# Compressed blocks laid side by side in SBUF, written by ScalarE and VectorE instead of by DMA, in a hybrid attention decoder block

## The chip, the core and the metric

The kernel runs on one NeuronCore of a Trainium2 chip. The metric is the device time of one execution in microseconds (us), from start to end of the program. Of the engines, TensorE (PE) multiplies matrices, and its weight loads are listed apart as PEld; VectorE (DVE), ScalarE (ACT) and GpSimd (POOL) do elementwise work; SyncE (SP) issues most DMAs. A few runs of the same kernel are taken and their median is given; one further execution is profiled.

## The reference

One decoder layer for 512 tokens of width 1024: an RMS norm, one input projection, an attention group and a gated short convolution group side by side, an output projection, and then a gated MLP with a short convolution. The attention group has 8 query heads, 2 key/value groups and three branches. The part that the change touches is the compressed branch: keys and values are cut into 31 overlapping blocks of 32 tokens (a new one every 16 tokens), a position table `pe` is added, and each block goes through a small MLP whose first layer has 32 x 64 inputs.

```python
def compress_kv(kv, pe, w1, w2):
    B, S, G, dh = kv.shape
    n_cmp = (S - L_CMP) // S_CMP + 1                      # 31
    idx = jnp.arange(n_cmp)[:, None] * S_CMP + jnp.arange(L_CMP)[None, :]
    blk = kv[:, idx] + pe[None, None, :, None, :]
    blk = blk.transpose(0, 3, 1, 2, 4).reshape(B, G, n_cmp, L_CMP * dh)
    return jax.nn.gelu(blk @ w1, approximate=True) @ w2

    kc = compress_kv(k_c, pe_k, wk1, wk2)
    vc = compress_kv(v_c, pe_v, wv1, wv2)
    logits_c = jnp.einsum('bgrsd,bgnd->bgrsn', qg, kc) * scale + tab[:, :, t5_bucket(dist_c)]
    p_c = masked_softmax(logits_c, dist_c >= 0)
    o_c = jnp.einsum('bgrsn,bgnd->bgrsd', p_c.astype(vc.dtype), vc)
```

All inputs and outputs are float32.

## The kernel before

Float32 precision is kept with pairs: `split` (L132) writes a tile as `hi`, a copy rounded to float32r by ACT (L134), and `lo`, the rest, by a subtraction on DVE (L135). A product is then the sum of hi times hi, lo times hi and hi times lo. Weights arrive through `Stream` (L55): a load of 512 KB on SP's queue into one of three `raw` tiles (L73), then a split on ACT (L85) and DVE (L88) into one of four `ring` tiles.

The kernel's order is: a start-up that normalizes and projects keys, values and two query groups; then the attention steps with projection steps filled in between (`fill`, L564), in the order written out in `ORDER` (L44); the output projection; the MLP's up-projection (line `pu`) and down-projection (line `z`). In the filled part `c0` and `c1` project the 128 columns (2 groups x 64) of keys and values for compression; `q2` and `q3` are query projections; `h0` to `h7` are the first layer of the compression MLP; `g`, `x` and `b` belong to the short convolution; `s` is the second layer of the compression MLP. The instructions of an engine run in a fixed order, which the framework sets when the program is built.

The code around the change:

- `blocks(kv, p)` (L425) runs after `c0` and after `c1`. `normed` (L370) takes the projection out of PSUM into a tile of tag `t2` (three buffers), on DVE (L372). One `split` of 128x512 makes `hl`, hi and lo, in two more `t2` buffers. Then eight DMAs on SP's queue (L435) copy pieces of `hl` into X, one for each half of a token pair (`lp`), group `g` and `s` (hi or lo). The last 16 tokens of group 0 don't go to X but to `tails`, by two small splits (L431).
- X holds, on partition `lp*64 + d`, value `d` of token `t + lp`, in the order kv, hi/lo, group, token: tokens side by side. Tokens `2*l2` and `2*l2 + 1` of a block lie on the two halves of the partitions, so that 16 steps of `l2` cover a block's 32 tokens.
- `hidden_steps(c)` (L443) does the first layer: for each `l2` and `kv` the stationary operand `xs` (L453) is taken from X: 4 (hi/lo, group) times 32 (block) columns, 16 elements apart. The moving operand is 256 columns of the weights, first hi, then lo. That is 16 x 2 x 2 = 64 matmuls (L457), each with its own weight load, all into the bank `ph`.
- The position table is carried as a 32nd block of group 0, whose result is later added as a bias (`peb`, L477). In the first half of the steps the places of this block hold `pes[:, :, :, :8]`; before `c == 4`, `halves()` (L437) puts the tails back and writes the second half of the table into the beginning of group 1.

Of the kernel before, what the change touches and what calls it, by code (L numbers as in the profile page):

```python
# [22 lines left out]
F32R = mybir.dt.float32r  # L23
# [4 lines left out]
S = 512  # L28
D = 1024
P = 128  # L30
NT = S // P
KT = D // P
HD = 64
NH = 8
NG = 2
NB = 32
NCMP = 31
# [13 lines left out]
def f32(ap):  # L51
    return ap.bitcast(F32)
# [58 lines left out]
def block_kernel(ctx: ExitStack, tc: tile.TileContext, a, out):  # L111
    nc = tc.nc
# [4 lines left out]
    const = ctx.enter_context(tc.tile_pool(name="const", bufs=1))  # L117
# [14 lines left out]
    def split(hi, lo, src):  # L132

        act(hi, src, AF.Copy)  # L134
        nc.vector.tensor_tensor(lo, src, f32(hi), op=ALU.subtract)  # L135
# [13 lines left out]
    for what in ORDER.split():  # L149
        name, _, count = what.partition(":")  # L150
# [24 lines left out]
    opool = opool_cm.__enter__()  # L175
    ph1_cm = tc.tile_pool(name="ph1", bufs=1)
    ph1 = ph1_cm.__enter__()
# [168 lines left out]
    for n in range(2):  # L346
        nc.sync.dma_start(UR[:, 4 * n:4 * n + 4, :], bass.AP(tensor=vd.tensor, offset=vd.offset + n * 4 * 640,
                                                             ap=[[1, P], [640, 4], [1, S]]))
# [21 lines left out]
    def normed(p, name):  # L370
        t = t2(name)[:, :S]
        nc.vector.tensor_tensor(t, p, Rb, op=ALU.mult)  # L372
        return t
# [38 lines left out]

    X = opool.tile([P, 4 * 1024 + 16], F32R, tag="o16", name="X")
    Xv = X[:, :4096].rearrange("p (v s g t) -> p v s g t", v=2, s=2, g=NG)
    nc.gpsimd.memset(f32(X[:, 4096:]), 0.0)
    pes = const.tile([P, 2, 2, 16], F32R, name="pes")  # L420
    split(pes[:, :, 0], pes[:, :, 1], peT)
    tails = const.tile([P, 2, 2, 8], F32R, name="tails")
    nc.vector.tensor_copy(Xv[:, :, :, 0, 496:512:2], f32(pes[:, :, :, :8]))

    def blocks(kv, p):  # L425
        p = normed(p, f"ct{kv}")
        hl = [ph1.tile([P, 520], F32R, tag="t2", bufs=3, name=f"x{s}{kv}")[:, :S] for s in range(2)]
        split(hl[0], hl[1], p)
        for lp in range(2):
            half = slice(lp * HD, (lp + 1) * HD)  # L430
            split(tails[half, kv, 0], tails[half, kv, 1], p[:HD, 496 + lp:512:2])  # L431
            for g in range(NG):
                n = S - lp if g else 496
                for s in range(2):
                    nc.sync.dma_start(f32(Xv[half, kv, s, g, :n]), f32(hl[s][g * HD:(g + 1) * HD, lp:lp + n]))  # L435

    def halves():  # L437
        nc.vector.tensor_copy(Xv[:, :, :, 0, 496:512:2], f32(tails))
        nc.vector.tensor_copy(Xv[:, :, :, 1, 0:16:2], f32(pes[:, :, :, 8:]))

    phs = {}

    def hidden_steps(c):  # L443

        if c == 0:
            phs[0] = mm_bank("ph")
        w = W.next()
        if c == 4:
            halves()
        for l in range(2):  # L450
            l2 = 2 * c + l
            for kv in range(2):
                xs = bass.AP(tensor=X.tensor, offset=X.offset + kv * 2048 + 2 * l2, ap=[X.ap[0], [512, 4], [16, 32]])  # L453
                for s in range(2):
                    cc = slice(l * 512 + kv * 256, l * 512 + kv * 256 + 256)

                    MM(phs[0][:, kv * 256:kv * 256 + 256], xs, w[:, s, cc],  # L457
                       start=l2 == 0 and kv == 0 and s == 0, stop=l2 == 15 and kv == 1 and s == 1)
            yield
# [37 lines left out]
    def c_steps(kv):  # L497
        p = mm_bank(f"pp_c{kv}")
        yield from proj_steps(p, W.next())
        blocks(kv, p)  # L500
# [39 lines left out]
    def b_steps(c):  # L540
# [3 lines left out]
        split(oTc[:, 0, c, :], oTc[:, 1, c, :], ct[c])  # L544

    kinds = {"q": q_steps, "h": hidden_steps, "g": g_steps, "x": x_steps, "b": b_steps}

    def work():
# [28 lines left out]
    def compressed_softmax(i):  # L577
# [10 lines left out]
        m = const.tile([P, NH], F32, tag="cm", bufs=2, name=f"cm{i}")  # L588
        nc.vector.tensor_reduce(m, zv, axis=AX.X, op=ALU.min)
        nc.vector.tensor_tensor(zv, zv, m[:, :, None].to_broadcast([P, NH, nv]), op=ALU.subtract)  # L590
        act(zv, zv, AF.Exp, scale=-1.0)
        sm = const.tile([P, NH], F32, tag="csm", bufs=2, name=f"csm{i}")
        nc.vector.tensor_reduce(sm, zv, axis=AX.X, op=ALU.add)
        nc.vector.reciprocal(sm, sm)
# [263 lines left out]
    for n, m in enumerate(UP):  # L858
# [7 lines left out]
        if m >= NF:  # L866
            f = m - NF
# [97 lines left out]
```

## Time and profile before

| what | us |
|---|---|
| median of 3 runs (632.74 to 636.84) | 634.15 |
| the profiled execution | 633.81 |
| its span, from the first to the last instruction | 632.0 |
| PE busy | 622.0 |
| weight loads busy | 517.8 |
| DVE busy | 372.9 |
| ACT busy | 305.3 |
| POOL busy | 42.8 |

The mean granted TensorE clock is 0.996 of full speed. Busy times of PE and of its weight loads overlap each other. Matmuls are pipelined: one begins before the one ahead of it ends, so that the time that a matmul costs in a row of them is the distance from start to start and not its duration. A window is a stretch of the span, in us from its start. In the chain of waits, work is followed back from the last instruction, at each step to what released it.

### The profile page before, as it was taken

The numbers are of one execution on the slowest core, as the hardware profiler recorded it, in microseconds if no ns is written. First come the engines' busy times: TensorE is split into PE (matmuls) and PEld (weight loads), VectorE is DVE, ScalarE is ACT, GpSimd is POOL, SyncE is SP. The second block draws the span as 40 slices with busy tenths as digits, with TensorE's granted clock in tenths as the row PEclk, the third lists the DMA queues.
The fourth block names the chain that finished last, engine by engine and source line by source line (L and its number), as shares of the span: only waits on it lengthen the run. The fifth ranks groups of instructions, "written<-read, shape, count | busy, mean of one in ns | idle before, by whom it ended". The sixth has DMA issues, their size and how long they took to land.

```text
span 632.0 us, 8054 instructions
## 1 busy us (share of the span) xinstructions
PE 622.0 (98%) x2980; PEld 517.8 (82%) x2980; DVE 372.9 (59%) x665; ACT 305.3 (48%) x562; POOL 42.8 (7%) x90
## 2 busy tenths in 40 slices
PE   8999999999999999999999999999999999999995
PEld 7888898878878788898888888888888888888884
DVE  4677756689988746647656566665656542222224
ACT  5757735589998736346433444343443321222212
POOL 1200002003020203200000000000000000000001
PEclk9999999999999999999999999999999999999998
DMA  8976555201112573014222222332332223222103
GB/s 312 337 207 200 146 186 167 69 18 41 45 42 76 169 263 134 1 34 133 101 100 96 87 91 96 100 101 100 101 100 101 98 102 98 92 87 90 67 10 124
DMA packets 26295, 71.45 MB, mean 113 GB/s; under 512 B 3368, under 2 KB 8040, under 8 KB 26256
## 3 DMA queue, kind: packets, MB, share of 16 engines
q1 hardware_dynamic: 25968, 70.65, 33.9%
q8 instruction: 23, 0.38, 0.2%
q10 hardware_dynamic: 288, 0.29, 0.1%
q14 instruction: 16, 0.13, 0.1%
HBM read 64.88 MB, written 2.12 MB: 106 GB/s over the span
## 4 chain that ended last, share of the span: by engine, by line
PE 94%; DVE 2%; DMA 1%; ACT 1%; POOL 0%; SPq 0%; issue 0%; DVEq 0%; POOLq 0%; ACTq 0%
PE pu L170 13%; PE pu L171 13%; PE pu L169 13%; PE z L770 6%; PE z L769 6%; PE z L771 6%; PE sc L620 3%; PE y L770 2%; PE y L771 2%; PE y L769 2%; PE tr L649 2%; PE ph L457 2%; PE o L657 1%; PE o L658 1%; PE pcg L169 1%; PE pcg L171 1%
## 5 line engine op out<-in xcount | busy, mean ns | idle before, releaser
L169 PE MATMUL pu<-h2T,w_u 128*128 128x512 f32 (+1 forms) x384 | 142.8, 372 | 0.0
L170 PE MATMUL pu<-h2T,w_u 128*128 128x512 f32 (+1 forms) x384 | 142.6, 371 | 0.0
L171 PE MATMUL pu<-h2T,w_u 128*128 128x512 f32 (+1 forms) x384 | 142.6, 371 | 0.0
L169 PEld LDWEIGHTS pu<-h2T,w_u 128*128 128x128 f32 x384 | 72.3, 188 | 12.6
L170 PEld LDWEIGHTS pu<-h2T,w_u 128*128 128x128 f32 x384 | 72.3, 188 | 12.5
L171 PEld LDWEIGHTS pu<-h2T,w_u 128*128 128x128 f32 x384 | 72.3, 188 | 12.4
L853 DVE SCALAR_TENSOR_TENSOR cv<-pu,ffnw,cv 128x511 f32<-128x511 f32 x44 | 32.9, 749 | 70.2 <-ACT cv L852 70.2
L88 DVE TENSOR_TENSOR w_d<-raw_d,w_d 128x1024 fp32r<-128x1024 f32 x22 | 26.9, 1224 | 72.8 <-ACT w_d L85 72.8
L769 PE MATMUL z<-w_d,aT 128*128 128x512 f32 x176 | 68.5, 389 | 0.0
L770 PE MATMUL z<-w_d,aT 128*128 128x512 f32 x176 | 68.5, 389 | 0.0
L771 PE MATMUL z<-w_d,aT 128*128 128x512 f32 x176 | 68.5, 389 | 0.0
L852 ACT ACTIVATE cv<-pu,ffnw 128x512 f32<-128x512 f32 x44 | 30.3, 688 | 64.0 <-PE pu L171 63.9
L85 ACT ACTIVATE w_d<-raw_d 128x1024 fp32r<-128x1024 f32 x22 | 23.3, 1059 | 75.2 <-PE z L771 75.2
L88 DVE TENSOR_TENSOR w_u<-raw_u,w_u 128x1024 fp32r<-128x1024 f32 x44 | 53.4, 1216 | 5.9 <-ACT w_u L85 5.8
L85 ACT ACTIVATE w_u<-raw_u 128x1024 fp32r<-128x1024 f32 x44 | 46.2, 1052 | 6.6 <-PE pu L171 6.3
L626 ACT ACTIVATE P<-P,mins 128x512 f32<-128x512 f32 (+3 forms) x64 | 35.4, 554 | 7.8 <-DVE mins L624 7.4
L769 PEld LDWEIGHTS z<-w_d,aT 128*128 128x128 f32 x176 | 33.0, 188 | 6.9
L771 PEld LDWEIGHTS z<-w_d,aT 128*128 128x128 f32 x176 | 33.0, 188 | 6.9
L770 PEld LDWEIGHTS z<-w_d,aT 128*128 128x128 f32 x176 | 33.0, 188 | 6.7
L134 ACT ACTIVATE aT<-cv 128x512 fp32r<-128x512 f32 x22 | 13.9, 631 | 49.4 <-DVE cv L870 49.4
L854 DVE SCALAR_TENSOR_TENSOR cv<-pu,ffnw,cv 128x510 f32<-128x510 f32 x44 | 32.8, 748 | 1.5
L624 DVE CUSTOM_DVE_ANT_0 P<-sc,UR 128x512 f32<-128x512 f32 (+3 forms) x64 | 30.1, 482 | 2.6 <-PE sc L620 1.7
(221 smaller groups left out, 1111.3 us busy)
## 6 DMA issues: line engine op xcount, KB each, us to landing
raw_u<-in_w_u SPq DMA_DIRECT2D x44, 512.0 KB, 3.2
raw_d<-in_w_d SPq DMA_DIRECT2D x22, 512.0 KB, 3.2
raw_c<-in_w_c SPq DMA_DIRECT2D x8, 512.0 KB, 3.3
raw_o<-in_w_o SPq DMA_DIRECT2D x8, 512.0 KB, 3.4
xT<-in_xT SPq DMA_DIRECT2D x8, 256.0 KB, 5.1
xt<-in_x SPq DMA_DIRECT2D x4, 512.0 KB, 4.8
raw_q<-in_w_t SPq DMA_DIRECT2D x4, 512.0 KB, 6.3
UR<-vd SPq DMA_DIRECT2D x2, 1024.0 KB, 8.3
```

What stands on the lines that cost most here:

```text
L85: self.nc.scalar.activation(t[:, 0, c:c + step], self.raws[n][:, c:c + step], AF.Copy)
L88: eng.tensor_tensor(t[:, 1, cs], self.raws[n][:, cs], f32(t[:, 0, cs]), op=ALU.subtract)
L169: MM(dst, wh, xh, start=first, stop=False)
L170: MM(dst, wh, xl, start=False, stop=False)
L171: MM(dst, wl, xh, start=False, stop=last)
L626: act(v, v, AF.Exp, bias=m, scale=-1.0, accum_out=self.sums[:, r, b:b + 1])
L769: MM(y, oh_, w[:, 0, cs], start=first, stop=False)
L770: MM(y, ol_, w[:, 0, cs], start=False, stop=False)
L771: MM(y, oh_, w[:, 1, cs], start=False, stop=last)
L852: act(t, pu, AF.Copy, scale=ffnw[:, m, 2:3])
L853: nc.vector.scalar_tensor_tensor(t[:, 1:], pu[:, :S - 1], ffnw[:, m, 1:2], t[:, 1:], op0=ALU.mult, op1=ALU.add)
L854: nc.vector.scalar_tensor_tensor(t[:, 2:], pu[:, :S - 2], ffnw[:, m, 0:1], t[:, 2:], op0=ALU.mult, op1=ALU.add)
```

## The change

X gets the shape 16 x 2 x 2 x 2 x 32: position `l`, kv, hi/lo, group, block. The 128 columns that one stationary load takes are neighbours. `blocks` writes X by four splits, one for each half of the token pair and each group: ACT writes hi, DVE writes lo, 64 partitions x 496 elements each (16 positions x 31 blocks). The source `v` is read from the normed tile with a step of 2 elements over positions and 16 elements over blocks, the blocks innermost. The tiles `hl` and `tails`, the sixteen DMAs and `halves` are gone. Block 31 of group 0 holds the position table from the start, written by two casts; block 31 of group 1 is set to zero by POOL.

```diff
-    X = opool.tile([P, 4 * 1024 + 16], F32R, tag="o16", name="X")
-    Xv = X[:, :4096].rearrange("p (v s g t) -> p v s g t", v=2, s=2, g=NG)
-    nc.gpsimd.memset(f32(X[:, 4096:]), 0.0)
+    X = opool.tile([P, 16, 2, 2, NG, 32], F32R, tag="o16", name="X")
+    nc.gpsimd.memset(f32(X[:, :, :, :, 1, NCMP]), 0.0)
     pes = const.tile([P, 2, 2, 16], F32R, name="pes")
     split(pes[:, :, 0], pes[:, :, 1], peT)
-    tails = const.tile([P, 2, 2, 8], F32R, name="tails")
-    nc.vector.tensor_copy(Xv[:, :, :, 0, 496:512:2], f32(pes[:, :, :, :8]))
+    for kv in range(2):
+        nc.vector.tensor_copy(X[:, :, kv, :, 0, NCMP], f32(pes[:, kv].rearrange("p s l -> p l s")))
 
     def blocks(kv, p):
         p = normed(p, f"ct{kv}")
-        hl = [ph1.tile([P, 520], F32R, tag="t2", bufs=3, name=f"x{s}{kv}")[:, :S] for s in range(2)]
-        split(hl[0], hl[1], p)
         for lp in range(2):
             half = slice(lp * HD, (lp + 1) * HD)
-            split(tails[half, kv, 0], tails[half, kv, 1], p[:HD, 496 + lp:512:2])
             for g in range(NG):
-                n = S - lp if g else 496
-                for s in range(2):
-                    nc.sync.dma_start(f32(Xv[half, kv, s, g, :n]), f32(hl[s][g * HD:(g + 1) * HD, lp:lp + n]))
-
-    def halves():
-        nc.vector.tensor_copy(Xv[:, :, :, 0, 496:512:2], f32(tails))
-        nc.vector.tensor_copy(Xv[:, :, :, 1, 0:16:2], f32(pes[:, :, :, 8:]))
+                src = p[g * HD:(g + 1) * HD, :]
+                v = bass.AP(tensor=src.tensor, offset=src.offset + lp, ap=[src.ap[0], [2, 16], [16, NCMP]])
+                split(X[half, :, kv, 0, g, :NCMP], X[half, :, kv, 1, g, :NCMP], v)
 
@@ hidden_steps(c)
-        if c == 4:
-            halves()
         for l in range(2):
             l2 = 2 * c + l
             for kv in range(2):
-                xs = bass.AP(tensor=X.tensor, offset=X.offset + kv * 2048 + 2 * l2, ap=[X.ap[0], [512, 4], [16, 32]])
+                xs = X[:, l2, kv].rearrange("p s g n -> p (s g n)")
```

## Rows read from the trace of the kernel before

**Rows 1.** The page: busy us by engine; the chain by engine.

```profile
PE 622.0 (98%) x2980; PEld 517.8 (82%) x2980; DVE 372.9 (59%) x665; ACT 305.3 (48%) x562; POOL 42.8 (7%) x90
...
PE 94%; DVE 2%; DMA 1%; ACT 1%; POOL 0%; SPq 0%; issue 0%; DVEq 0%; POOLq 0%; ACTq 0%
```

**Rows 2.** Windows: length, busy PE, PEld, DVE, ACT, POOL (instructions), clock, DMA share, GB/s.

```profile
53.60:68.00 14.40, 14.40 (x70) 11.91 (x69) 9.98 (x22) 9.13 (x20) 0.71 (x1) 1.00 0.77 202
...
68.00:103.00 35.00, 35.00 (x162) 31.40 (x162) 22.26 (x29) 16.57 (x21) 5.37 (x7) 1.00 0.54 165
```

**Rows 3.** The tile X: ns min/median/max, first and last start, form.

```profile
L457 PEld LDWEIGHTS ph<-w_c,X x64: 293/314/318, 67.8 to 102.5; 128*128 128x128 f32 x64
...
L435 SPq DMA_DIRECT2D X<-x x16: 462/594/604, 54.3 to 68.2; - x16
...
L438 DVE CAST X<-tails x1: 183/183/183, 85.4 to 85.4; 128x32 fp32r<-128x32 f32 x1
```

**Rows 4.** Groups by line, weight loads, 68 to 103 us: busy us, mean ns.

```profile
L457 PEld LDWEIGHTS ph<-w_c,X 128*128 128x128 f32 x64 | 15.0, 311 | 0.4
L169 PEld LDWEIGHTS pcg<-hT,w_tg 128*128 128x128 f32 x9 | 1.7, 194 | 0.3
L170 PEld LDWEIGHTS pcg<-hT,w_tg 128*128 128x128 f32 x9 | 1.7, 188 | 0.3
```

**Rows 5.** Chain, 68 to 103 us: shares by line; pieces (start us, us, what).

```profile
by line: PE ph L457 37.9%; PE pxt L171 5.3%; PE pcg L171 5.3%; PE pxt L170 5.3%; PE pbg L169 5.3%; PE pbg L171 5.3%; PE pcg L170 5.3%; PE pcg L169 5.2%; PE pbg L170 5.2%; PE pxt L169 5.2%; PE pp_q L171 3.3%; PE pp_q L170 2.6%; PE pp_q L169 
...
68.17 0.35 PE ph L457 x2
...
72.67 1.23 PE ph L457 x6
...
74.84 1.67 PE ph L457 x8
...
101.40 1.67 PE ph L457 x8
```

**Rows 6.** Timeline of PE, early up-projection, 256 columns: start us, us, what.

```profile
263.72 0.28 PE L171 MATMUL pu<-h2T,w_u 128*128 128x256 f32 x1
...
265.52 0.28 PE L171 MATMUL pu<-h2T,w_u 128*128 128x256 f32 x1
```

**Rows 7.** Groups by line, DVE and ACT, 48 to 70 us: busy us, mean ns.

```profile
L135 DVE TENSOR_TENSOR x<-ct,x 128x512 fp32r<-128x512 f32 x2 | 1.4, 692 | 1.0 <-ACT x L134 1.0
L135 DVE TENSOR_TENSOR tails<-ct,tails 64x8 fp32r<-64x8 f32 x4 | 0.6, 158 | 0.1
...
L134 ACT ACTIVATE x<-ct 128x512 fp32r<-128x512 f32 x2 | 1.2, 616 | 0.0
L134 ACT ACTIVATE tails<-ct 64x8 fp32r<-64x8 f32 x4 | 0.8, 202 | 0.0
```

**Rows 8.** Groups by line, DVE, 80 to 215 us: busy us, mean ns.

```profile
L586 DVE TENSOR_TENSOR zc<-pcs,UR 128x248 f32<-128x248 f32 x1 | 0.6, 607 | 2.6 <-PE pcs L574 2.6
L587 DVE TENSOR_TENSOR zc<-pcs,zc 128x248 f32<-128x248 f32 x1 | 0.4, 412 | 0.0
...
L586 DVE TENSOR_TENSOR zc<-pcs,UR 128x56 f32<-128x56 f32 x1 | 0.3, 252 | 1.1 <-PE pcs L574 1.1
L587 DVE TENSOR_TENSOR zc<-pcs,zc 128x56 f32<-128x56 f32 x1 | 0.2, 211 | 0.0
```

**Rows 9.** Timeline of DVE: start us, us, what.

```profile
59.51 0.68 DVE L135 TENSOR_TENSOR ptl<-tr,pth 128x512 fp32r<-128x512 f32 x1
...
65.60 1.22 DVE L88 TENSOR_TENSOR w_tg<-raw_tg,w_tg 128x1024 fp32r<-128x1024 f32 x1
...
90.90 1.22 DVE L88 TENSOR_TENSOR w_c<-raw_c,w_c 128x1024 fp32r<-128x1024 f32 x1 [2.96 <-ACT w_c L85]
```

**Rows 10.** Timeline of PE: start us, us, what.

```profile
64.10 0.39 PE L658 MATMUL o<-ptl,V 128*128 128x512 f32 x1
...
76.35 0.39 PE L169 MATMUL pcg<-hT,w_tg 128*128 128x512 f32 x1
...
96.82 1.84 PE L457 MATMUL ph<-w_c,X 128*128 128x256 f32 x8
```

## The prediction

> **What bounds the kernel now.** I read the page's busy times and its chain first. PE is busy 622.0 of 632.0 us, and PE makes up 94% of the chain that ended last [rows 1]. DVE and ACT, at 372.9 and 305.3 us, have room on average. So an edit pays here only where it shortens what PE itself does, or where it starves PE. Next come the windows around the compression: in the 14.4 us before the first hidden-layer matmul, and in the 35 us in which those matmuls run, PE is busy all the time [rows 2]. No DMA and no other engine stands in front of PE there, so the sixteen copies into X are hidden today: taking them away is worth nothing by itself.
>
> The view of the tile X shows what is not hidden. The 64 weight loads that read X take 314 ns at the median [rows 3]. In the same stretch the load of another 128x128 tile, with the projection's weights lying side by side, takes 194 ns on average against 311 ns for X, at an unchanged granted clock of 1.00 [rows 4, 2]. The line that reads X takes one element in sixteen, 64 bytes apart; every other load there reads neighbours. The chain of this stretch gives what the slow loads cost: L457 sets 37.9% of 35 us, that is 13.3 us. Piece by piece it is two matmuls in 0.35, six in 1.23 and seven runs of eight at 1.66 to 1.67 us, together 13.2 us, or 0.207 us for a matmul of 256 columns [rows 5]. The early up-projection has matmuls of the same 256 columns, each with its own contiguous load: fifteen steps from 263.72 to 265.52 us, 0.120 us each [rows 6]. Each X load thus holds PE some 0.087 us longer than a contiguous one would.
>
> **The change part by part.**
>
> The stationary read. X is stored so that the 128 columns of one load are neighbours. 64 matmuls at 0.120 us are 7.7 us against 13.3, a gain of 5.6 us, all on the path that sets the end. I take 0.120 because width, type and back-to-back loads are the same in both rows. As bounds: if the load stays slow for another reason the gain is nothing; I see no row with 256 columns that goes faster than 0.120, so 5.6 is the other end.
> [...]
>
> The write of the blocks. Before, each of the two tensors had one split of 128x512 and two small ones for the tails. On DVE the two tensors together are 1.4+0.6 = 2.0 us, on ACT 1.2+0.8 = 2.0 us [rows 7]. Now each has four splits of 64x496, eight on each engine. Their source is read every sixteenth element. From below: 496 contiguous elements, a little under the 0.692 and 0.616 us of the 512-wide rows, so 0.67 us on DVE and 0.60 on ACT. From above: the nearest row is a DVE operation that reads an SBUF operand with a step of sixteen elements, the bias add of L586, and beside it L587, the same shape without that step. At 248 elements they take 607 and 412 ns, at 56 elements 252 and 211 [rows 8]; the step costs (195-41)/192 = 0.80 ns for an element, 0.40 us for 496. That makes 1.07 us on DVE and, if ACT pays as much, 1.00 us there. I take the upper ends, since L586 is the row with the same step.
> Eight times 1.07 is 8.6 us, so DVE gets 6.6 us more; ACT gets 8.0-2.0 = 6.0 us more. Both lie before the first hidden matmul. There DVE is busy 9.98 and ACT 9.13 of 14.40 us [rows 2]. DVE comes to 16.6, that is 2.2 us more than the stretch holds; ACT to 15.1, or 0.7 more. At the flat price DVE comes to 13.3 and fits. The stall is thus between 0 and 2.2 us.
> The cover is this. The first PE work behind DVE's delayed queue is a PV matmul at 64.10 us, whose operand is done at 59.51+0.68 = 60.19 [rows 9, 10]: 3.9 us to spare, more than the delay. And DVE's work in that stretch is not all due in it: the split of w_tg, 1.22 us at 65.60, is first read at 76.35 [rows 9, 10], so it can come after the blocks. What is exposed is the first hidden matmul itself, which reads a tile into which all splits write. I put the stall at 0.4 us.
> [...]
>
> The DMAs. Sixteen issues on SP's queue go, with the waits on ACT and DVE in front of them [rows 3]. What is queued behind them on SP are weight loads, which can only start earlier. The third buffer of t2 comes free sooner too. Neither reaches PE, which never waited in these stretches [rows 2]: 0.
>
> The pe blocks. One cast more at the start, two casts of 0.18 us at 85 us gone [rows 3], a larger memset on POOL, which is almost idle [rows 1]. No PE time was lost on the late casts [rows 2], and none is counted: 0, give or take 0.2 us for the cast at the start.
>
> What comes next. With the hidden matmuls 5.6 us shorter, weights are wanted faster: 29.4 us instead of 35. DVE has 22.3 and ACT 16.6 us of work there [rows 2], and a weight tile whose split starts at 90.90 and lasts 1.22 us is used at 96.82 [rows 9, 10], 4.7 us ahead. The supply holds. After that PE is the bound up to the end, so what is won stays won.
>
> The sum against the profiled execution: 633.81 us, of which 632.0 are the span, minus 5.6, plus 0.4, is 628.6. The profiled execution lies 0.34 us under the median of the runs, 634.15; set against that median the forecast is 629.0 us, 0.8% faster.
>
> **The rivals.**
>
> The load stays as it is: something other than the step makes the X loads slow. Then the gain is nothing and the time 634.2, or up to 636 with the stall. Against it: in the same stretch X is the only tile loaded with such a step, and the loads beside it take 188 to 194 ns [rows 4]. Chance 0.06. [...]
>
> The writes starve PE beyond my bounds: the end on the other side. Place: ACT, DVE and the first hidden matmul. DVE's other work before it is 9.98-2.0 = 8.0 us; with a price p for each split the stall is 8.0+8p-14.4. It eats the whole 5.6 when p reaches 1.50 us, and the kernel is 1% slower at 2.3 us. That would need a step to cost twice what L586 shows [rows 8], or an order on DVE that leaves the blocks to the last. Chance 0.05 for slower than before (0.04 for more than 1%), and 0.09 for a stall between 2.2 and 5.6 us, 631 to 634.
>
> More than forecast: the order of work on each engine is made anew, and PE's small waits in the attention that follows get fewer. PE is idle 10 us in all [rows 1], so some 2 us at most, below 627.0. Chance 0.06.
>
> **How the numbers follow.** The forecast, a gain of 5.6 less a stall of 0 to 2.2 us, has 0.74; its own range is 627.0 to 631.0, where the runs of the kernel before spread from 1.4 us below their median upwards. About 1% is what a measurement of this kernel tells from no change; the line is at 627.8. The forecast's middle is 1.2 us above that line, and of its 0.74 I give 0.22 to times under it; with the 0.06 for more, faster has 0.28. Slower by over 1% has 0.04, and the rest, 0.68, is within 1%. The range 627.0 to 633.0 takes in the forecast and most of the longer stall, 0.81.
>
> **What would show it.** In the trace after, X loads near 190 ns and the pieces of eight hidden matmuls near 0.96 us instead of 1.67 prove the gain. The eight splits on DVE show their price, 0.67 or 1.07 us, and the chain's first hidden piece, at 68.17 us before [rows 5], shows the stall. The forecast is wrong if X loads stay over 300 ns, if PE waits for the blocks by more than 2 us, or if PE's waits between 105 and 215 us change by as much as the gain.

## The result and the profile after

The changed kernel takes 627.06 us (median of five runs, 626.68 to 628.9); the kernel before, with two more runs than at first, 632.74 us. The ratio is 0.9913, interval 0.9896 to 0.9929: 0.9% faster, 5.7 us between the medians. The forecast was 629.0 us, within 627.0 and 633.0, and 0.8% faster. The median lies 0.06 us above the lower end of that range, and two of the five runs lie below it.

The page of the changed kernel, busy us by engine and the chain by engine; it answers to [rows 1]:

```profile
PE 614.7 (98%) x2980; PEld 511.0 (82%) x2980; DVE 377.6 (60%) x666; ACT 311.6 (50%) x564; POOL 44.8 (7%) x90
...
PE 81%; DVE 6%; issue 5%; ACT 3%; DMA 2%; POOL 2%; SPq 0%; DVEq 0%; POOLq 0%; ACTq 0%
```

PE is busy 7.3 us less with the same 2980 matmuls, and weight loads 6.8 us less. DVE has 4.7 us more and ACT 6.3, for the most part from their eight splits. PE's share of the chain falls from 94% to 81%: the chain now leaves PE in the middle, because PE waits there.

The tile X after (ns min/median/max, first and last start, form), for [rows 3, 4, 7]:

```profile
L445 PEld LDWEIGHTS ph<-w_c,X x64: 187/189/192, 66.6 to 97.7; 128*128 128x128 f32 x64
...
L134 ACT ACTIVATE X<-ct x8: 1054/1066/1081, 52.7 to 62.9; 64x496 fp32r<-64x496 f32 x8
L135 DVE TENSOR_TENSOR X<-ct,X x8: 1002/1012/1051, 53.8 to 64.3; 64x496 fp32r<-64x496 f32 x8
```

The load of X falls from 314 to 189 ns. The price went over to the two engines that now read with the step: a split of 496 elements costs ACT 1.07 us and DVE 1.01 us, where 512 neighbours cost 0.62 and 0.69 [rows 7].

The windows after (columns as in [rows 2]):

```profile
53.60:68.00 14.40, 14.40 (x73) 11.93 (x72) 13.76 (x22) 12.42 (x17) 0.00 (x0) 1.00 0.22 73
68.00:80.00 12.00, 10.53 (x57) 8.54 (x56) 9.78 (x14) 9.97 (x17) 1.57 (x2) 1.00 0.33 105
```

Ahead of the hidden matmuls DVE is nearly full, 13.8 of 14.4 us, and ACT has 12.4. PE has no gap in that stretch; it gets one in the next, 1.5 us.

PE's timeline there, and at the two later places that matter (start us, us, what, idle time and what ended it):

```profile
66.80 0.64 PE L445 MATMUL ph<-w_c,X 128*128 128x256 f32 x4
...
72.13 0.39 PE L646 MATMUL o<-ptl,V 128*128 128x512 f32 x1
73.77 0.51 PE L645 MATMUL o<-pth,V 128*128 128x512 f32 x1 [1.25 <-ACT pth L134]
74.49 0.50 PE L646 MATMUL o<-ptl,V 128*128 128x512 f32 x1 [0.22 <-DVE ptl L135]
74.83 1.11 PE L445 MATMUL ph<-w_c,X 128*128 128x256 f32 x8
...
78.53 1.12 PE L445 MATMUL ph<-w_c,X 128*128 128x256 f32 x8
79.48 0.40 PE L169 MATMUL pcg<-hT,w_tg 128*128 128x512 f32 x1
...
100.50 0.39 PE L171 MATMUL pcg<-hT,w_tg 128*128 128x512 f32 x1
101.59 0.46 PE L459 MATMUL pg<-ident,g 64*128 64x64 f32 x4 [0.70 <-DVE g L455]
```

Three things stand in it. Eight hidden matmuls take 0.95 us from start to start (78.53 to 79.48) instead of the 1.67 of [rows 5]; over all 64 that is 7.6 us instead of 13.3. PE loses 2.0 us at 72 us, in the PV matmuls: from 72.13 to 74.83 it takes 2.70 us for three steps, and three steps of 0.23, the distance between the matmuls of 512 columns just ahead (71.44 to 72.13 in three), are 0.70. Of that, 1.25 us is a wait for ACT and 0.22 us one for DVE; the steps behind the two waits are longer too. And PE loses 0.8 us at the transposes `pg` of the second layer, where it waits for DVE's sum: they start 1.09 us after the matmul ahead of them, and 0.32 us in the kernel before.

Of the two spans, 632.0 and 625.3 us, about 1.1 us of the distance is not the change's. The first projection of the keys starts at 21.0 us in the profiled execution of before and at 20.0 us after. The twelve other profiles below lie at 19.3 to 20.5; that of a kernel whose start differs from before by one memset alone lies at 19.5. The profiled execution of before also lies 1.1 us above its median (633.81 against 632.74).

Following the same matmuls through both traces, with that start taken off, the rest of the distance, 5.7 us, comes to: 5.6 us won at the hidden matmuls, 2.0 and 0.8 us lost at the two waits, 0.5 us won in the attention, 1.1 us won in the output projection, 1.1 us won after the last matmul, and some 0.2 us in small pieces. The gains in the attention, in the output projection and at the end have no term in the forecast's sum.

Of the 0.5 us in the attention, 0.4 is one wait, from the list of PE's waits before:

```profile
PE o L677 <- DMA bd<-zt: 0.2, 1, 0.2
```

The two steps around it, from the matmul ahead to the second product with `bd`, take 0.89 us before and 0.47 after, where the list has no such wait. With the read alone and with the writes alone, the first two experiments below, the wait is still there (0.3 and 0.2 us). What takes it away is open. The experiments take up the output projection and the end.

### The profile page after: what moved, and what is told of

The parts are those of the page before. It is cut to its first block, busy times and chain, and to the rows that moved or that the text cites. A ratio compares the mean times of both kernels' runs of the same rounds, so it can differ in the third digit from the quotient of the medians.

```text
span 625.3 us, 8021 instructions
## 1 busy us (share of the span) xinstructions
PE 614.7 (98%) x2980; PEld 511.0 (82%) x2980; DVE 377.6 (60%) x666; ACT 311.6 (50%) x564; POOL 44.8 (7%) x90
## 4 chain that ended last, share of the span: by engine, by line
PE 81%; DVE 6%; issue 5%; ACT 3%; DMA 2%; POOL 2%; SPq 0%; DVEq 0%; POOLq 0%; ACTq 0%
PE pu L169 13%; PE pu L170 13%; PE pu L171 13%; PE z L759 6%; PE z L757 6%; PE z L758 6%; PE tr L637 2%; PE y L759 2%; PE y L758 2%; PE y L757 2%; PE sc L608 2%; PE o L645 1%; PE o L646 1%; DMA xt<-in_x 1%; PE pxt L169 1%
```

## The experiments

**The read alone.** The first kernel keeps the old writing and changes how a load takes its columns; one more memset at the start sets 16 columns in each row of X that the loads now reach.

```diff
+    nc.gpsimd.memset(f32(Xv[:, :, :, :, 496:]), 0.0)
...
-                xs = bass.AP(tensor=X.tensor, offset=X.offset + kv * 2048 + 2 * l2, ap=[X.ap[0], [512, 4], [16, 32]])
+                xs = X[:, kv * 2048 + l2 * 128:kv * 2048 + l2 * 128 + 128]
```

> The kernel before, with one edit: the 128 columns of a stationary load are taken as neighbours out of the old X (so the hidden layer gets the wrong tokens; the work is of the same size), and 16 more columns per row of X are zeroed at the start. The splits, the sixteen DMAs and the late casts stay. The load theory: X loads of 188 us/1000 each, 0.120 us per hidden matmul, 5.6 us off PE between 66 and 103 us, no stall at the PV matmuls near 72 us; perhaps 0.7 us lost where the second layer waits for its sum. So 626.5 to 628 us where the kernel before has 632.5. The rival, that the copies and their waits were what cost: no change, 632 to 633 us. If the output projection is faster in the changed kernel because of where its operands lie in SBUF, that 1 us is missing here, and its matmuls stay at 0.231 to 0.233 us.

Measured: 627.69 us (627.51 to 628.5), ratio 0.9914 (0.9899 to 0.993), and the loads:

```profile
L458 PEld LDWEIGHTS ph<-w_c,X x64: 187/189/192, 66.2 to 95.5; 128*128 128x128 f32 x64
L458 PE MATMUL ph<-w_c,X x64: 277/283/364, 66.5 to 95.6; 128*128 128x256 f32 x64
L436 SPq DMA_DIRECT2D X<-x x16: 461/594/630, 52.8 to 67.0; - x16
```

With all sixteen copies in place the kernel gains as much as the whole change does. So the load theory holds and the copies were hidden. PE has no wait at the PV matmuls here and the 0.7 us at `pg`; the output projection and the end are as in the kernel before. So the equal gain has other parts: neither the 2.0 us that the splits cost nor the 2.2 us won in those two places.

**The writes alone.** The second kernel is the changed one with the old step put back on the read.

```diff
-                xs = X[:, l2, kv].rearrange("p s g n -> p (s g n)")
+                xs = bass.AP(tensor=X.tensor, offset=X.offset + kv * 2048 + l2, ap=[X.ap[0], [512, 4], [16, 32]])
```

> The changed kernel, with one edit: the stationary columns are again taken 16 elements apart out of the new X (wrong tokens and positions for the hidden layer, work of the same size). The writes by ACT and DVE stay, the DMAs stay gone. The load theory: X loads of 314 ns again, 0.207 us per hidden matmul, plus the stall that the writes cost at the PV matmuls, 1 to 1.5 us: 632.5 to 634 us, no faster than the kernel before. The rival, that taking away the copies and their waits is what gains: 627 to 629 us.

Measured: 631.83 us (631.19 to 636.06), ratio 0.9986 (0.9964 to 1.0009). The loads are back at 314 ns, and the gain is gone: the interval of the ratio includes 1. The waits of PE:

```profile
PE o L645 <- ACT pth L134: 1.4, 1, 1.4
```

The splits cause the PV wait by themselves; with the slow hidden matmuls there is no wait at `pg`. The time came out 0.7 us under what I expected: this kernel too has the faster output projection and the shorter end, 2.2 us together, which the expectation did not count.

**What makes a split dear.** The third kernel reads 496 neighbours in place of every sixteenth element.

```diff
-                v = bass.AP(tensor=src.tensor, offset=src.offset + lp, ap=[src.ap[0], [2, 16], [16, NCMP]])
+                v = bass.AP(tensor=src.tensor, offset=src.offset, ap=[src.ap[0], [NCMP, 16], [1, NCMP]])
```

> The changed kernel, with one edit: the splits read 496 neighbouring tokens of the normed tile instead of every sixteenth (wrong tokens in X; the writes and the shape stay). If the source's step is the price of the splits: 0.67 us each on DVE and 0.60 on ACT instead of 1.01 and 1.07, the 1.4 us wait of the PV matmuls at 72 to 74.5 us shrinks to under 0.3, and the kernel takes 625.0 to 626.2 us against 627.0. If the price is in the way X is written (31 neighbours, then 1 KB on), the splits stay at 1.0 us and the time at 627.

Measured: 624.84 us (624.53 to 624.88), ratio 0.9865 (0.9848 to 0.9883).

```profile
L134 ACT ACTIVATE X<-ct x8: 606/617/618, 52.2 to 59.7; 64x496 fp32r<-64x496 f32 x8
L135 DVE TENSOR_TENSOR X<-ct,X x8: 657/670/674, 52.9 to 61.2; 64x496 fp32r<-64x496 f32 x8
```

It is the source's step: 0.45 us for a split on ACT, 0.34 on DVE. X is written in runs of 31 as before, and that costs nothing that shows: 617 and 670 ns for 496 elements, against 616 and 692 for 512 neighbours [rows 7]. The PV wait is gone, and 2.2 us with it by the medians, 2.0 us between the same matmuls in the two traces. That is 0.2 us under what I expected, where I had counted the loss at 1.4.

**The step of a load, measured.** A load of 128 columns was taken with steps of 2, 4, 8 and 16 elements, 16 loads each.

```diff
-                xs = X[:, l2, kv].rearrange("p s g n -> p (s g n)")
+                xs = bass.AP(tensor=X.tensor, offset=X.offset + kv * 2048 + l2, ap=[X.ap[0], [(2, 4, 8, 16)[c // 2], 128]])
```

> The changed kernel, in which the stationary columns are taken 2 elements apart in the first two weight tiles of the hidden layer, 4 in the next two, then 8, then 16 (wrong tokens for the hidden layer, work of the same size): 16 loads at each step. If a load costs by the 16-byte lines that it opens, steps of 4, 8 and 16 elements all cost as much as 16 did, 314 ns, and a step of 2 lies near 189. If the price grows with the distance, 4 and 8 lie in between. With 0.087 us for each load at the full price, 48 such loads give 4.2 us back: about 631 us.

Measured: 630.17 us, one run. Groups of weight loads (busy us, mean ns) in four windows, 65 to 76 us for step 2, 77 to 85 for 4, 86 to 94 for 8, 95 to 105 for 16:

```profile
L445 PEld LDWEIGHTS ph<-w_c,X 128*128 128x128 f32 x16 | 2.4, 197 | 0.2
...
L445 PEld LDWEIGHTS ph<-w_c,X 128*128 128x128 f32 x16 | 3.9, 325 | 0.1
...
L445 PEld LDWEIGHTS ph<-w_c,X 128*128 128x128 f32 x16 | 4.0, 335 | 0.1
...
L445 PEld LDWEIGHTS ph<-w_c,X 128*128 128x128 f32 x16 | 3.7, 311 | 0.1
```

8 bytes apart costs 197 ns, hardly more than neighbours, 189; 16, 32 and 64 bytes apart cost 325, 335 and 311. From 16 to 64 bytes the price does not grow with the distance. So the first case of the expectation came; that lines of 16 bytes are the reason is not shown, the four steps only place the rise between 8 and 16 bytes. Equal counts of 128 columns take 189 to 335 ns here. The time is 0.8 us under the 631 expected: the hidden matmuls take 4.8 us more than in the changed kernel, but PE no longer loses the 0.8 us at `pg`.

**A version without the dear reads.** The normalization, one DVE operation for each tensor, writes its tile in the order parity, position, block; the four splits then read neighbours, and X has the same values.

```diff
-        p = normed(p, f"ct{kv}")
+        t = t2(f"ct{kv}")[:, :S]
+        by_token = lambda ap: ap.rearrange("p (m j a) -> p m j a", j=8, a=2)
+        nc.vector.tensor_tensor(t.rearrange("p (a j m) -> p m j a", a=2, j=8), by_token(p), by_token(Rb), op=ALU.mult)
...
-                v = bass.AP(tensor=src.tensor, offset=src.offset + lp, ap=[src.ap[0], [2, 16], [16, NCMP]])
+                v = bass.AP(tensor=src.tensor, offset=src.offset + lp * 256, ap=[src.ap[0], [1, 2], [32, 8], [1, NCMP]])
...
```

> The changed kernel, in which the normalization itself (L372, one operation for each of the two tensors) writes its tile in the order parity, position, block, so that the four splits read runs of 31 neighbours. Same values in X. If the source's step is what makes a split cost 1.01 to 1.07 us: splits of 0.67 us on DVE and 0.62 on ACT; the normalization goes from 0.69 to between 0.7 and 1.1 us, depending on what a write with a step costs; the wait of the PV matmuls at 72 to 74 us goes from 1.4 us to under 0.3, and the time from 627.0 to 625.0 to 625.8 us. If the step only moves its price to the write, at more than 1.5 us for the normalization, part of the wait stays: 626 to 627 us.

Measured: 625.44 us (624.88 to 626.37), ratio 0.9887 (0.9871 to 0.9904). Splits of 0.62 us on ACT and 0.67 on DVE. DVE's timeline:

```profile
51.72 1.10 DVE L425 TENSOR_TENSOR ct<-pp_c,Rb 128x512 f32<-128x512 f32 x1
```

Writing with a step costs DVE 0.41 us for 512 elements (1.10 against 0.69), about what reading with it does (0.34 for 496). But it is paid once for a tensor instead of four times on each of two engines. PE is busy 11.97 of the 12 us from 68 to 80.

**And one step more ahead of `pg`.** The same, with the order `s:1 g1:5 s:1 g1:2 s:1 g1:1` in place of `s:1 g1:4 s:1 g1:3 s:1 g1:1`.

> As e5_permuted_norm, and one projection step of g1 (three matmuls) more ahead of the transposes of the second layer, which wait 0.6 to 0.8 us for DVE's sum in the changed kernel at 100.5 us. If that wait is only a lack of work to put in front, the step's 0.68 us fills it: 0.5 to 0.7 us faster than e5_permuted_norm, 624.3 to 625.2 us. If PE waits for something that is itself held up by PE's earlier steps, nothing is won: as e5_permuted_norm.

Measured: 624.45 us (623.84 to 624.52), ratio 0.9869 (0.9854 to 0.9883), 1.0 us under the last. The three matmuls fill the gap: `pg` starts at 99.78, 0.4 us after the matmul ahead of it, and PE's wait for DVE is gone from the list of waits. In the traces 0.66 us of the gain lie there, from `pg` to the first product of the second layer; the rest lies ahead of it, where the order of PE's work is the same in both. This version is the fastest of those that compute what the reference does, 2.6 us under the changed kernel and 8.4 under the kernel before.

**The output projection.** Its matmuls come every 0.233 us before and every 0.227 after, with the same operands. Before, then after (timelines of PE; seven rows from first to last):

```profile
224.10 0.40 PE L771 MATMUL y<-w_o,oTc 128*128 128x512 f32 x1
...
225.50 0.40 PE L771 MATMUL y<-w_o,oTc 128*128 128x512 f32 x1
```

```profile
219.29 0.39 PE L759 MATMUL y<-w_o,oTc 128*128 128x512 f32 x1
...
220.66 0.39 PE L759 MATMUL y<-w_o,oTc 128*128 128x512 f32 x1
```

Six matmuls take 1.40 us before and 1.37 after; over the 192 that is about 1.0 us. What the change does to them is to move them: the tile of X is 64 bytes shorter, and two more tiles share its size. The next kernel gives X its old size.

```diff
-    X = opool.tile([P, 16, 2, 2, NG, 32], F32R, tag="o16", name="X")
+    Xs = opool.tile([P, 4 * 1024 + 16], F32R, tag="o16", name="X")
+    X = Xs[:, :4096].rearrange("p (l k s g n) -> p l k s g n", l=16, k=2, s=2, g=NG)
```

> The changed kernel, with X in a tile of 4112 elements as before instead of 4096, so that the second buffer of its tag, and all that is laid out behind, lies 64 bytes further on. Nothing else changes. If the output projection's matmuls got faster, from 0.231 to 0.233 to 0.227 us, because of where their operands lie, they go back to 0.231 or more and the kernel loses 0.9 us, 628 us. If it was something else, the tile of 128 bytes that is gone from the constants or chance, they stay at 0.227 and the time at 627.

Measured: 628.72 us (627.89 to 629.75), ratio 0.9929 (0.9909 to 0.9949), and PE's timeline:

```profile
219.26 0.39 PE L759 MATMUL y<-w_o,oTc 128*128 128x512 f32 x1
...
220.66 0.39 PE L759 MATMUL y<-w_o,oTc 128*128 128x512 f32 x1
```

1.40 us for six again, and 1.0 us for the whole output projection. The place of the operands is worth 1 us here. Two more kernels ask which operand. In one X gets 4128 elements:

```diff
-    X = opool.tile([P, 16, 2, 2, NG, 32], F32R, tag="o16", name="X")
+    Xs = opool.tile([P, 4 * 1024 + 32], F32R, tag="o16", name="X")
+    X = Xs[:, :4096].rearrange("p (l k s g n) -> p l k s g n", l=16, k=2, s=2, g=NG)
```

> The changed kernel with X in a tile of 4128 elements: the second buffer of its tag lies 128 bytes further on than in the changed kernel, all that is behind it 256. Nothing else changes. If the output projection slows down when its operands lie off a multiple of 128 bytes, its matmuls stay at 0.227 us here, and the time at 627. If any shift does it, they take 0.231 to 0.233 us as in e4_old_slot, and the time is 628.

In the other, 128 bytes of padding stand behind the tiles of X's tag:

```diff
+    pad = opool.tile([P, 32], F32, tag="pad", bufs=1, name="pad")
+    nc.gpsimd.memset(pad, 0.0)
```

> The changed kernel with 128 bytes of padding behind the two buffers of X's tag and ahead of the pools that follow, and one more memset on POOL. X, oTc and oTn stay where they are; what the output projection reads from the last five of its weight tiles moves by 128 bytes, its first three weight tiles don't. If the place of those weights matters, the matmuls with oTn go from 0.227 to 0.231 to 0.233 us and those with oTc mostly stay at 0.227, 0.5 us in all. If only the place of oTc and oTn matters, all stay at 0.227.

Measured: 628.39 and 628.04 us, one run each. With the wider X the matmuls that load oTc go to 0.233 us and those that load oTn stay at 0.227; with the padding it is the other way about. The mean durations go with it: 395 to 401 ns with oTc and 390 to 392 with oTn in the wider X, 390 to 395 with oTc and 395 with oTn with the padding, 389 to 393 in the changed kernel. So a shift of 128 bytes slows one group when it moves the stationary operand (oTc, whose first three weight tiles stay in place) and the other when it moves the weights (those read with oTn). The wider X moves those weights by 256 bytes, and they don't get slower. What decides, these few shifts don't say. The padding did what its expectation says for the case that the place of the weights matters; the wider X did what neither of its two cases says, since only the matmuls with oTc slowed down.

**The end.** After the last matmul the kernel before runs 7.4 us and the changed one 6.3 us, and the instructions are the same. The span less the end of the last row of PE gives it; before, after:

```profile
624.25 0.39 PE L771 MATMUL z<-w_d,aT 128*128 128x512 f32 x1
```

```profile
618.62 0.39 PE L759 MATMUL z<-w_d,aT 128*128 128x512 f32 x1
...
q14 instruction: 15, 0.12, 0.1%
```

632.0 - 624.64 is 7.4, 625.3 - 619.01 is 6.3. The kernel with the read alone has the long end (7.4), all others so far the short one. The page counts the packets that fall into the span: the kernels with the long end have 16 in the queue q14, listed there as `instruction`, and those with the short end 15. The packet that makes the difference is in both traces. It starts 5.1 us after the last matmul in the kernel before, and 7.4 us after it in the changed one, behind the end of the span. My first thought was SP, whose program the copies made longer:

```diff
+    scr = dram.tile([16, NCMP], F32, name="scr")
...
                 split(X[half, :, kv, 0, g, :NCMP], X[half, :, kv, 1, g, :NCMP], v)
+                for s in range(2):
+                    n = kv * 8 + lp * 4 + g * 2 + s
+                    nc.sync.dma_start(scr[n:n + 1, :], f32(X[lp * HD:lp * HD + 1, 0, kv, s, g, :NCMP]))
```

> The changed kernel with sixteen small DMAs put back on SP's queue, two after each split of the blocks; each takes 31 elements of one partition of X to a scratch line in HBM that nobody reads. In the trace before, SP's last instructions are held until an instruction packet of its queue that starts 629.7 us into the span, and the end comes 7.4 us after the last matmul; in the changed kernel no such packet falls into the end, and it comes 6.3 us after. If what counts is how many instructions SP runs, the sixteen bring the packet back and the end to 7.4 us: 628.1 us against 627.0. If the end is shorter for another reason, it stays at 6.3 us and the time within 0.4 us of 627.0. The load theory expects the hidden matmuls at 0.120 us and the PV wait of about 1.4 us in both cases.

Measured: 628.0 us (626.89 to 630.07), ratio 0.9932 (0.991 to 0.9953); the end is 6.3 us and q14 has 15 packets. So it is not SP's count, and sixteen small DMAs cost nothing that shows in the trace: the span is 625.3 us with and without them, and the PV wait for ACT 1.1 us against 1.25. The 1.1 us between the two ends lie in SP's last long wait, 2.65 us in the kernel before and 1.54 in the changed one; that the packet is what ends it is not shown, nor that q14 is SP's queue. The median is 0.9 us higher, in runs that scatter over 3 us. Two more engines have programs that the change made shorter, POOL by three instructions and DVE by four.

```diff
+    nc.gpsimd.memset(mhalf, -0.5)
+    nc.gpsimd.memset(mhalf, -0.5)
+    nc.gpsimd.memset(mhalf, -0.5)
```

> The changed kernel with three more memsets on POOL at the start, of one value on each partition that is already there, so that POOL runs 133 instructions as in the kernel before and not 130. If the end after the last matmul is 1.1 us longer in the kernel before because POOL's program there ends just beyond what is fetched at once, the end is 7.4 us here, 628.2 us in all, with an instruction packet some 5.1 us after the last matmul. If not, the end stays at 6.3 us and that packet at 7.4 us.

```diff
+    nc.vector.memset(first, 0.0)
+    nc.vector.memset(first, 0.0)
+    nc.vector.memset(first, 0.0)
+    nc.vector.memset(first, 0.0)
```

> The changed kernel with four more memsets on DVE at the start, of one value on each partition that is already there, so that DVE runs 834 instructions as in the kernel before and not 830. If it is DVE's program that ends beyond what is fetched at once in the kernel before, the end is 7.4 us here instead of 6.3, 628.2 us in all. If not, it stays at 6.3 us, and the cause of the longer end is neither of the two counts.

Measured: 627.1 and 628.26 us, one run each. With POOL's three the end stays at 6.3 us. With DVE's four (span 626.5 us):

```profile
618.70 0.39 PE L763 MATMUL z<-w_d,aT 128*128 128x512 f32 x1
...
q14 instruction: 16, 0.13, 0.1%
```

626.5 - 619.09 is 7.4 us, and q14 has 16 packets in the span again. Four instructions on DVE, done in the first microseconds, cost 1.1 us at the end. Why is not shown: that a program ends beyond what is fetched at once was my guess in the last two expectations, and the traces have only the packet and its time. That the count on DVE decides is shown between these two counts: the three kernels with the long end run 834 instructions there, all with the short end 830 (with those that the page doesn't count).

## Why the prediction was right, and where it was not

The way and the size are right, and the time lies in the range, though 0.06 us from its lower end. In the ratio, 0.8% forecast and 0.9% measured, the agreement is better than the steps were; the last part of the sum below shows that this was luck.

*What bounds the kernel.* Right. PE sets the time, the copies were hidden, the loads of X were what could be won. The read alone gains 0.9% with all copies in place.

*The stationary read.* Right to the number: 0.120 us a matmul was taken from [rows 6], eight take 0.95 us, and the whole is 13.3 - 7.6 = 5.6 us.

*The price of the splits.* The row with the same step [rows 8] was the right one to lean on: 1.07 us forecast for DVE and 1.01 measured, 1.00 for ACT and 1.07 measured.

*The stall.* Here the step failed. I put 0.4 us, at the first hidden matmul, and DVE as the engine behind it. The hidden matmul did not wait. PE lost 2.0 us later, at the fourth pair of PV matmuls, first to ACT and then to DVE. I had looked at the first consumer behind the delayed queues, which had 3.9 us to spare [rows 9, 10], and taken it for the one that waits first. The fourth had 2.6 us, and both sides move towards it. The copy of the transposed chunk that those matmuls read, on ACT's timeline, and before also the matmul on PE's:

```profile
71.06 0.58 ACT L134 ACTIVATE pth<-tr 128x512 fp32r<-128x512 f32 x1
...
74.21 0.39 PE L657 MATMUL o<-pth,V 128*128 128x512 f32 x1
```

```profile
70.99 1.06 ACT L85 ACTIVATE w_c<-raw_c 128x1024 fp32r<-128x1024 f32 x1
72.42 0.72 ACT L614 ACTIVATE P<-P,mins 128x512 f32<-128x512 f32 x1 [0.37 <-DVE mins L612]
73.05 0.19 ACT L614 ACTIVATION_READ_ACCUMULATOR P<-P,mins 128x1 f32 x1
73.14 0.58 ACT L134 ACTIVATE pth<-tr 128x512 fp32r<-128x512 f32 x1
```

The copy comes 2.1 us later by the clock of the span, and 3.1 us with the different starts of the two executions taken off. It stands behind a weight split and an exponential that are themselves late; the exponential waits 0.37 us for DVE. And PE comes earlier, ready at 72.36 instead of 74.21 us, which is 0.8 us with the starts taken off, because the eight hidden matmuls ahead of the pair are short. Together that is 3.9 us against 2.6 to spare. The size, 2.0 us, is inside the bounds of 0 to 2.2 that I had from DVE's sum, but near their upper end and not at 0.4; it just doesn't pass the 2 us that I had named as a sign of being wrong.

*What comes next.* "The supply holds. After that PE is the bound up to the end, so what is won stays won" was wrong by 0.8 us. I had tested the weights, and they do hold. What I left out is the second layer's sum, which no faster PE brings forward: DVE's timeline after shows it behind an operation that waits for POOL.

```profile
98.52 0.69 DVE L531 TENSOR_TENSOR ct<-pbg,ct 128x512 f32<-128x512 f32 x1 [1.34 <-POOL ct L506]
99.13 1.22 DVE L88 TENSOR_TENSOR w_tb<-raw_tb,w_tb 128x1024 fp32r<-128x1024 f32 x1
...
100.86 0.68 DVE L455 TENSOR_TENSOR g<-ph,g 64x512 f32<-64x512 f32 x1
```

*The DMAs and the casts at nothing.* Right for PE in the stretches that I looked at, and wrong for the whole kernel. The smaller tile moved the operands of the output projection, 1.1 us, and the shorter DVE program took 1.1 us off the end. Nothing in the rows that I had could have priced either.

So the sum that the runs show is -5.6 + 2.0 + 0.8 - 0.5 - 1.1 - 1.1, or -5.5, of the 5.7 us between the traces; the forecast had -5.6 + 0.4. PE lost 2.4 us more than forecast, and 2.7 us were won in places that had no term. That the two nearly cancel is luck. The number itself, 629.0, was 1.9 us high; of that 1.4 is the median that it was set against, 634.15 of three runs, where five give 632.74.

*The rivals.* The load that stays slow is excluded by the read alone. Writes that starve PE do exist, and take 2.0 us, within the bounds and far from the 5.6 that would decide. More than forecast did not come by its own sign, a time below 627.0. PE's waits in the attention did get fewer, as that rival says, but by 0.4 us; the larger gains came in the output projection and at the end.

## What to carry to other kernels

In this kernel a weight load of 128 float32r columns takes 311 to 335 ns instead of 189 when they lie 16 to 64 bytes apart, and a matmul of 256 columns doesn't hide that: it costs 0.207 us instead of 0.120 at 64 bytes. Lay the columns side by side, and let the engine that pays for the order pay once, before the work is copied, split or fanned out (here 0.41 us for a tensor on DVE, instead of 0.34 for each of its four splits on DVE and 0.45 on ACT). When PE gets faster in one place, go through every consumer behind the delayed queues, not only the first, and through the results that other engines deliver at their own pace; a step of filler work ahead of such a wait cost nothing here and won 0.66 us. A difference of 1 us in a kernel of 630 can be the place of a tile or four instructions more on another engine, so a change of layout is best tested against a version that only moves the tiles.

## What the hardware showed that I had not expected

Two effects had no part in my reasoning. The output projection's matmuls of 512 columns come every 0.227 us or every 0.233 us, depending on where in SBUF their operands lie, with shifts of 64 or 128 bytes; that is 1.0 us for 192 matmuls. And four more instructions on DVE at the start of the program, 834 instead of 830, lengthen its end by 1.1 us, 7.4 instead of 6.3, and the queue q14 then has 16 packets in the span instead of 15.
